# Rotary embedding in a hybrid decoder trunk: blocks of rows moved to other partitions by ScalarE copies instead of transfers

## The chip, the cores and the metric

The program runs on one core of a Trainium2 chip. The core has five engines, each with a queue of its own that is worked through in order: TensorE (PE in the profile: matmuls, and PEld for its weight loads), VectorE (DVE), ScalarE (ACT), GpSimd (POOL) and SyncE (SP). An engine's queue can hold instructions that issue a transfer (DMA); here SP issues the loads of weights and ACT issues the small transfers inside the on-chip memory. On-chip data lie in 128 partitions (rows). The metric is the device time of one execution in microseconds (us), as the median of several runs.

## The reference

The reference is two layers of a decoder trunk with three branches side by side, on 512 tokens of width 1024 in float32. Each layer norms its input, projects it, runs the three branches (a chunked state-space scan, a latent attention, a gated delta rule), merges them through gates and an output projection, and ends in a feed-forward block. The change touches the latent attention alone:

```
def apply_rope(t, cos, sin):
    t1, t2 = tf[..., :half], tf[..., half:]          # half = 32 of 64 rotary channels
    return concat([t1 * cos - t2 * sin, t2 * cos + t1 * sin])

q = (rmsnorm(cq) @ w_uq).reshape(B, S, 8, 128 + 64)  # 8 heads, 128 plain and 64 rotary channels
q_nope, q_pe = split(q);  q_pe = apply_rope(q_pe, cos, sin)
k_nope, v = split(rmsnorm(ckv) @ w_ukv);  k_pe = apply_rope(k_rope, cos, sin)   # one k_pe for all heads
sc = einsum(q_nope, k_nope) + einsum(q_pe, k_pe)     # scaled, causal, then softmax and the product with v
```

## The kernel before

**Layout.** The attention works on transposed tiles: channels on the 128 partitions, the 512 tokens along the row. Every matmul operand is kept as a high and a low part (`hi` rounded to the matmul's input type, `lo` the rest), and each product is three matmuls (lines 181 to 183). ACT makes `hi` with a cast (line 159 for weights, line 256 for values out of PSUM), DVE makes `lo` with a subtraction (lines 160 and 257).

**The stage.** In each of the two layers the attention begins after the projections of the compressed query and key/value (`latent`, whose casts are line 260 and whose scaling is line 495), and runs over four head pairs `hp` (lines 540 to 651). The 64 rotary channels of the two heads of a pair lie together in one tile of 128 partitions: head 0 in partitions 0 to 63, head 1 in 64 to 127. A pair goes through these steps:

- `dense_F(q_weights(), ...)`, line 558: queries of the pair in three PSUM banks, `pp` being the rotary one. ACT scales it into `qp` (line 575), and the plain ones into `qh` (line 568).
- `rope(qp)`, line 576, gives `qr`, the rotated query.
- `qd` (lines 578 to 580) is `qr` with its two halves of 64 partitions exchanged: two transfers.
- `qps[j]`, for each head j of the pair, holds the rounded query of this head in both halves of the partitions: its own half is cast from `qr` (line 584), the other half from `qd` (line 586). `qpl[j]` holds the low part in its own half (DVE, line 585) and zero in the other.
- Keys `kh`, `kl` and values `vh`, `vl` of the pair (lines 587 to 596): matmuls into PSUM, then casts on ACT (line 256) and subtractions on DVE (line 257), which set the PSUM banks free. There are four banks of the kind `acc`, shared with the next pair's queries and with the other stages.
- For each head, four score blocks of 128 tokens: three plain matmuls (lines 607 to 609), the rotary matmul of `qps[j]` with `kps` (line 610), that of `qpl[j]` with `kph` (line 611), and the mask (line 612). `kps` holds the high part of the rotated key in partitions 0 to 63 and its low part in 64 to 127, so line 610 computes two products at once; this is why the query has to lie in both halves. Then the maximum (line 616), the exponential (line 619), transposes (line 629), and the products with the values (lines 645 to 647) into `yt`, whose cast is `yh` (line 256).

**The key.** Before the pairs, the 64 rotary channels of the shared key `smT` are doubled into `kd` (lines 520 to 522, two transfers), rotated by `rope(kd)` (line 523), and split into `kph` and `kps` (lines 526 to 528).

**`rope`**, lines 509 to 518: `sw_` is the source with neighbouring blocks of 32 partitions exchanged, made by four transfers (line 513); then DVE computes `ta = src * cosT`, `sw_ = sw_ * sinT` and their sum (lines 515 to 517). It runs five times in a layer.

**Buffers.** `kd`, `sw_`, `ta` and `qd` are tiles of a pool `mix` of eight buffers, which the probabilities of the attention (lines 632 and 633) use too.

**Order.** The kernel's text gives no order between engines, and not the final order on an engine. A planner simulates the program with costs of its own and puts each instruction into its engine's queue when it takes it to be ready, the earlier one in the text first; blocks under `high_priority` count as earlier in the text than they stand. The waits between engines follow from the data. So the transfers of lines 513, 522 and 580 stand in ACT's queue between casts, where the planner put them, and an instruction of that queue that has to wait holds up what is behind it.

Of the kernel before, what the change touches and what calls it, by code (L numbers as in the profile page):

```python
# [10 lines left out]
F32 = mybir.dt.float32  # L11
# [9 lines left out]
P = 128  # L21
S = 512
# [37 lines left out]
def hybrid_kernel(ctx, tc, a, out, depth=2, taps=None):  # L60
    nc = tc.nc
    pe, act, dve, pool, sync = nc.tensor, nc.scalar, nc.vector, nc.gpsimd, nc.sync
    uid = itertools.count()

    def mk(pl, shape, dt, tag, bufs=None):
        return pl.tile(shape, dt, tag=tag, name=f"{tag}_{next(uid)}", bufs=bufs)
# [5 lines left out]
    def f32(ap):  # L72
        return ap.bitcast(F32)
# [12 lines left out]
    lp = ctx.enter_context(tc.tile_pool(name="lp", bufs=1))  # L86
# [76 lines left out]
    def weights(w2d, c0, n, K, hold=None):  # L163

        kt = min(1024 // n, K // P)
        step = 512 // n
        for k0 in range(0, K // P, kt):  # L170
            raw = mk(wp, [P, kt * n], F32, "wraw", 2)
            sync.dma_start(raw.rearrange("p (k n) -> p k n", n=n),
                           w2d[k0 * P : (k0 + kt) * P, c0 : c0 + n].rearrange("(k p) n -> p k n", p=P))
            for q in range(0, kt, step):
                hi, lo = split_half(raw[:, q * n : (q + step) * n], hold and hold[k0 + q])
                v = lambda x: x.rearrange("p (k n) -> p k n", n=n)
                yield k0 + q, v(hi), v(lo)
# [158 lines left out]
    for ly in range(depth):  # L336
# [32 lines left out]
        smT = mk(ml, [96, S], F32, "qp")  # L369
# [139 lines left out]
        def rope(src):  # L509

            sw_ = mk(lp, [P, S], F32, "mix", 8)
            for i in range(4):
                act.dma_start(sw_[32 * i : 32 * i + 32], src[32 * (i ^ 1) : 32 * (i ^ 1) + 32])
            ta = mk(lp, [P, S], F32, "mix", 8)
            dve.tensor_tensor(ta, src, cosT, ALU.mult)
            dve.tensor_tensor(sw_, sw_, sinT, ALU.mult)
            dve.tensor_tensor(ta, ta, sw_, ALU.add)
            return ta

        kd = mk(lp, [P, S], F32, "mix", 8)  # L520
        for i in range(2):
            act.dma_start(kd[64 * i : 64 * i + 64], smT[:64])
        kpe = rope(kd)
        kph = mk(ml, [P, S], F32R, "kph")
        kps = mk(ml, [P, S], F32R, "kps")
# [14 lines left out]
        for hp in range(4):  # L540
# [33 lines left out]
            qp = mk(ml, [P, S], F32, "qp")  # L574
            act.mul(qp, pp, scale)
            qr = rope(qp)

            qd = mk(lp, [P, S], F32, "mix", 8)
            for i in range(2):
                act.dma_start(qd[64 * i : 64 * i + 64], qr[64 * (1 - i) : 64 * (1 - i) + 64])  # L580
            qps = [mk(ml, [P, S], F32R, f"qps{j}") for j in range(2)]
            for j in range(2):
                half, other = (slice(64 * i, 64 * i + 64) for i in (j, 1 - j))
                act.copy(qps[j][half], qr[half])
                dve.tensor_tensor(qpl[j][half], qr[half], f32(qps[j][half]), ALU.subtract)
                act.copy(qps[j][other], qd[other])
            wkv = list(weights(a["mla_w_ukv"][ly], hp * 512, 512, 256))
            with tc.high_priority(30):
                ks = head_tiles(dense_F(wkv, [slice(0, P), slice(256, 256 + P)], 256, ckh, ckl), "k")
# [684 lines left out]
```

## Time and profile before

| | |
|---|---|
| median of 3 runs | 2353.61 us (2350.84 to 2354.39) |
| profiled execution | 2356.2 us |
| its span, from the first to the last instruction | 2354.4 us |
| mean granted TensorE clock | 0.998 of full speed |
| PE busy | 2309.5 us |
| DVE busy | 1608.8 us |
| ACT busy | 1154.9 us |
| attention of layer 0 and of layer 1, about | 60 to 205 us and 1222 to 1365 us of the span |

The profile shows one execution. An instruction is named by engine, line, operation and `out<-in` by tile names. A row of a timeline has its start and its duration in us, and in brackets how long the engine was idle before it and who released it. ACTq rows are instructions that ACT's sequencer handles itself, such as issuing a transfer. In the chain that ended last, each row is a start, a length and what the time was spent on. In a row for a line of the kernel, the three durations are the smallest, the median and the largest in ns. Matmuls are pipelined, so the busy time of PE says that it was not waiting, not that it ran at its peak.

### The profile page before, as it was taken

The page shows a single profiled execution, that of the slowest core. Times are in us where ns is not written, and L with a number is a line of the kernel's source. Part 1 is how long each engine was busy: PE and PEld are TensorE (multiplying, and loading weights), DVE is VectorE, ACT ScalarE, POOL GpSimd, SP SyncE. Part 2 cuts the span into 40 slices and gives each one's busy share as a digit, 9 for nine tenths or more (in the row PEclk, how much of TensorE's full clock was granted, in tenths as well). Part 3 has the DMA queues.
Part 4 walks back from the last instruction along what each step waited for, and adds up shares of the span by engine and source line. Part 5 has one row for each costly group of instructions (what it writes and reads, how often), then busy time and mean ns, then how long its engine had stood idle before and what let it go on. Part 6 is the DMA issues. An engine that isn't in the chain of part 4 may idle for free.

```text
span 2354.4 us, 32073 instructions
## 1 busy us (share of the span) xinstructions
PE 2309.5 (98%) x11972; PEld 1897.4 (81%) x11972; DVE 1608.8 (68%) x3184; ACT 1154.9 (49%) x2305; POOL 58.4 (2%) x76
## 2 busy tenths in 40 slices
PE   8999999999999999999999999999999999999998
PEld 7778788878887888888887787888888878888886
DVE  6776756775675458767757767667756645677668
ACT  6665434534453345544656553444435534455545
POOL 0000000000000000000000000000000000000000
PEclk9999999999999999999999999999999999999999
DMA  4222232252222443233132222323422224333231
GB/s 136 85 63 72 66 96 72 76 148 72 72 63 72 143 152 101 71 125 117 50 99 65 72 81 63 93 69 99 126 79 65 63 81 157 129 108 107 90 108 45
DMA packets 194172, 215.16 MB, mean 91 GB/s; under 512 B 32352, under 2 KB 153696, under 8 KB 194016
## 3 DMA queue, kind: packets, MB, share of 16 engines
q1 hardware_dynamic: 190496, 207.87, 29.0%
q10 hardware_dynamic: 3520, 5.25, 0.9%
q8 instruction: 94, 1.54, 0.3%
q14 instruction: 62, 0.51, 0.1%
HBM read 200.50 MB, written 7.34 MB: 88 GB/s over the span
## 4 chain that ended last, share of the span: by engine, by line
PE 90%; DVE 5%; DMA 2%; ACT 1%; issue 1%; POOL 1%; SPq 0%; DVEq 0%; POOLq 0%; ACTq 0%
PE acc L181 23%; PE acc L182 23%; PE acc L183 22%; PE sm L181 2%; PE sm L183 2%; PE sm L182 2%; PE sm L724 1%; DVE wlo L160 1%; PE sm L629 1%; PE yt L182 1%; PE yt L183 1%; PE yt L181 1%; PE sm L989 1%; DMA mix<-mix 1%; PE sm L461 1%
## 5 line engine op out<-in xcount | busy, mean ns | idle before, releaser
L160 DVE TENSOR_TENSOR wlo<-wraw,whi 128x512 fp32r<-128x512 f32 x552 | 378.3, 688 | 404.8 <-ACT whi L159 397.7
L159 ACT CAST whi<-wraw 128x512 fp32r<-128x512 f32 x552 | 342.0, 621 | 624.5 <-PE acc L182 406.6
L181 PE MATMUL acc<-xh,whi 128*128 128x512 f32 (+1 forms) x1184 | 462.1, 391 | 2.2 <-DVE vl L257 2.2
L183 PE MATMUL acc<-xh,wlo 128*128 128x512 f32 (+1 forms) x1184 | 459.3, 388 | 0.0
L182 PE MATMUL acc<-xl,whi 128*128 128x512 f32 (+1 forms) x1184 | 459.3, 388 | 0.0
L181 PEld LDWEIGHTS acc<-xh,whi 128*128 128x128 f32 x1184 | 222.8, 189 | 44.4 <-DVE vl L257 2.8
L182 PEld LDWEIGHTS acc<-xl,whi 128*128 128x128 f32 x1184 | 223.0, 188 | 42.6 <-issue 1.0
L183 PEld LDWEIGHTS acc<-xh,wlo 128*128 128x128 f32 x1184 | 222.9, 188 | 41.9 <-issue 0.5
L181 PE MATMUL acc<-yh,whi 128*128 128x512 f32 x384 | 153.1, 402 | 0.0
L182 PE MATMUL acc<-yl,whi 128*128 128x512 f32 x384 | 152.3, 397 | 0.0
L183 PE MATMUL acc<-yh,wlo 128*128 128x512 f32 x384 | 151.4, 394 | 0.0
L183 PE MATMUL acc<-whi,xl 128*128 128x512 f32 (+1 forms) x384 | 144.0, 375 | 0.0
L181 PE MATMUL acc<-whi,xh 128*128 128x512 f32 (+1 forms) x384 | 143.4, 375 | 0.0
L182 PE MATMUL acc<-wlo,xh 128*128 128x512 f32 (+1 forms) x384 | 143.2, 373 | 0.0
L665 DVE SCALAR_TENSOR_TENSOR cva<-acc,pc,cva 128x511 f32<-128x511 f32 (+2 forms) x168 | 120.1, 742 | 16.7 <-ACT cva L661 9.5
L159 ACT CAST whi<-wr 128x512 fp32r<-128x512 f32 x128 | 79.5, 621 | 68.2 <-PE acc L183 32.7
L182 PE MATMUL acc<-wlo,yh 128*128 128x512 f32 x256 | 99.7, 390 | 0.0
L181 PE MATMUL acc<-whi,yh 128*128 128x512 f32 x256 | 99.7, 389 | 0.0
L183 PE MATMUL acc<-whi,yl 128*128 128x512 f32 x256 | 99.7, 389 | 0.0
L160 DVE TENSOR_TENSOR wlo<-wr,whi 128x512 fp32r<-128x512 f32 x128 | 85.8, 685 | 12.5 <-ACT whi L159 11.7
L181 PEld LDWEIGHTS acc<-yh,whi 128*128 128x128 f32 x384 | 71.6, 188 | 16.9 <-ACT yh L260 2.2
L182 PEld LDWEIGHTS acc<-yl,whi 128*128 128x128 f32 x384 | 72.2, 188 | 16.0 <-issue 1.9
(381 smaller groups left out, 4601.3 us busy)
## 6 DMA issues: line engine op xcount, KB each, us to landing
wraw<-in_w_in_dram SPq DMA_DIRECT2D x148, 512.0 KB, 3.6
wraw<-in_w_up_dram SPq DMA_DIRECT2D x64, 512.0 KB, 3.6
wr<-in_w_down_dram SPq DMA_DIRECT2D x32, 1024.0 KB, 5.0
wraw<-in_w_mla_out_dram SPq DMA_DIRECT2D x16, 512.0 KB, 3.4
wraw<-in_w_ssd_out_dram SPq DMA_DIRECT2D x16, 512.0 KB, 3.4
wraw<-in_w_gdn_out_dram SPq DMA_DIRECT2D x16, 512.0 KB, 3.3
wraw<-in_w_out_dram SPq DMA_DIRECT2D x16, 512.0 KB, 3.6
wraw<-in_mla_w_uq_dram SPq DMA_DIRECT2D x16, 384.0 KB, 3.4
```

The lines of the kernel that those rows point to most:

```text
L159: act.copy(hi, raw)
L160: dve.tensor_tensor(lo, raw, f32(hi), ALU.subtract)
L181: pe.matmul(o, ah, bh, start=start, stop=False, skip_group_check=more)
L182: pe.matmul(o, ah, bl, start=False, stop=False, skip_group_check=more)
L183: pe.matmul(o, al, bh, start=False, stop=stop, skip_group_check=more)
L461: pe.matmul(ps, w, cum[1][:, t].rearrange("p i l -> p (i l)"), start=True, stop=True)
L629: pe.transpose(ps[:, n : n + P], pn[t][:, kb * P : (kb + 1) * P], ident)
L665: dve.scalar_tensor_tensor(acc[:, d:], ps[:, : S - d], taps_[3 - d], acc[:, d:], ALU.mult, ALU.add)
L724: pe.matmul(py[:, h * 64 : (h + 1) * 64], e2[h // 4][:, h % 4, :], xd[:, h * 64 : (h + 1) * 64], start=True, stop=True)
L989: pe.matmul(po[:, h * P : (h + 1) * P], pt_[:, h, :], vn[:, h * P : (h + 1) * P], start=True, stop=True)
```

## The change

The four transfers of the exchange in `rope`, and the two that double the key, become copies on ACT with the same source and destination. `qd` goes away with its two transfers; the other half of `qps[j]` is now cast straight from `qr`, from the half of the partitions in which the head lies to the other.

```diff
@@ rope(src)
             sw_ = mk(lp, [P, S], F32, "mix", 8)
             for i in range(4):
-                act.dma_start(sw_[32 * i : 32 * i + 32], src[32 * (i ^ 1) : 32 * (i ^ 1) + 32])
+                act.copy(sw_[32 * i : 32 * i + 32], src[32 * (i ^ 1) : 32 * (i ^ 1) + 32])
             ta = mk(lp, [P, S], F32, "mix", 8)
...
         kd = mk(lp, [P, S], F32, "mix", 8)
         for i in range(2):
-            act.dma_start(kd[64 * i : 64 * i + 64], smT[:64])
+            act.copy(kd[64 * i : 64 * i + 64], smT[:64])
         kpe = rope(kd)
...
             qr = rope(qp)
 
-            qd = mk(lp, [P, S], F32, "mix", 8)
-            for i in range(2):
-                act.dma_start(qd[64 * i : 64 * i + 64], qr[64 * (1 - i) : 64 * (1 - i) + 64])
             qps = [mk(ml, [P, S], F32R, f"qps{j}") for j in range(2)]
             for j in range(2):
                 half, other = (slice(64 * i, 64 * i + 64) for i in (j, 1 - j))
                 act.copy(qps[j][half], qr[half])
                 dve.tensor_tensor(qpl[j][half], qr[half], f32(qps[j][half]), ALU.subtract)
-                act.copy(qps[j][other], qd[other])
+                act.copy(qps[j][other], qr[half])
```

## The prediction

> **What bounds the kernel now.** I read the page first: the engines' busy time and the chain that ended last.
>
> ```profile
> span 2354.4 us, 32073 instructions
> PE 2309.5 (98%) x11972; PEld 1897.4 (81%) x11972; DVE 1608.8 (68%) x3184; ACT 1154.9 (49%) x2305; POOL 58.4 (2%) x76
> PE 90%; DVE 5%; DMA 2%; ACT 1%; issue 1%; POOL 1%; SPq 0%; DVEq 0%; POOLq 0%; ACTq 0%
> ```
>
> TensorE sets the time: 2354.4 - 2309.5 leaves 45 us in which it is idle. The change takes no matmul away, so all that it can win lies in those 45 us. Next I read the list of what PE waited for (total us, times, longest), then the five waits of its second line in PE's own timeline (start, duration; in brackets the idle time before and who ended it).
>
> ```profile
> PE sm L296 <- DVE xr L291: 9.0, 2, 8.7
> PE sm L610 <- ACT qps L586: 5.3, 5, 1.9
> PE acc L181 <- DVE vl L257: 3.6, 4, 1.1
> ...
> 115.69 0.38 PE L610 MATMUL sm<-kps,qps 128*128 128x256 f32 x1 [0.56 <-ACT qps L586]
> 146.72 0.39 PE L610 MATMUL sm<-kps,qps 128*128 128x256 f32 x1 [1.08 <-ACT qps L586]
> 1251.43 0.39 PE L610 MATMUL sm<-kps,qps 128*128 128x256 f32 x1 [1.13 <-ACT qps L586]
> 1282.63 0.39 PE L610 MATMUL sm<-kps,qps 128*128 128x256 f32 x1 [1.89 <-ACT qps L586]
> 1314.78 0.39 PE L610 MATMUL sm<-kps,qps 128*128 128x256 f32 x1 [0.62 <-ACT qps L586]
> ```
>
> The second-largest wait of the kernel is the one that the change touches: the rotary score matmul of a head pair waits for the copy that reads the doubled query. The five are 0.56 + 1.08 + 1.13 + 1.89 + 0.62 = 5.28 us. The chain, followed through these places, names what lay behind the copy.
>
> ```profile
> 110.73 4.28 DMA mix<-mix
> 140.10 5.21 DMA wraw<-in_w_in_dram
> 1246.18 4.56 DMA mix<-mix
> 1276.33 5.61 DMA mix<-mix
> 1308.61 4.75 DMA wraw<-in_w_in_dram
> ```
>
> Three times it is the doubling transfer itself, twice a load of weights. Why a load of weights: the last copy L586 then stands on ACT behind a weight cast L159 that waits for it. After the longest wait PE also ran at a lower clock; the table of windows (length, then PE's busy time and so on, the granted clock after POOL) shows it beside the same matmuls in layer 0.
>
> ```profile
> 1283.38:1287.13 3.75, 3.75 (x13) 2.50 (x12) 2.58 (x11) 1.60 (x6) 0.00 (x0) 0.54 0.00 0
> 116.63:118.78 2.15, 2.15 (x12) 1.50 (x12) 2.03 (x10) 1.60 (x6) 0.00 (x0) 1.00 0.00 0
> ```
>
> At 0.54 of full clock the stretch took 3.75 us, at 1.00 2.15 us: 1.60 us lost behind the 1.89 us idle, none behind the shorter ones. [...]
>
> **The change, part by part.** *Transfers removed:* per layer 2 (doubling the key) + 5 x 4 (swaps in the rotary helper) + 4 x 2 (doubled query) = 30, in two layers 60.
>
> ```profile
> q10 hardware_dynamic: 3520, 5.25, 0.9%
> L513 ACTq DMA_DIRECT2D mix<-qp x32: 514/552/613, 74.3 to 1335.3; - x32
> DMA to landing us min/median/max: 2.2/2.6/5.6
> 140.28 1.50 ACTq L580 DMA_DIRECT2D mix<-mix  x1
> ```
>
> These 60 are the whole queue q10 (5.25 MB). An issue holds ACT's sequencer for 552 ns (median); the landing row is that of the doubled query, median 2.6 us, worst 5.6 us, and the first of the two late weight loads (140.10 to 145.31) had one issued beside it at 140.28. *Copies added:* 22 per layer, 44 in all, of 32 or 64 partitions by 512.
>
> ```profile
> L447 ACT CAST cw<-wk x4: 615/616/617, 241.1 to 1410.1; 32x512 fp32r<-32x512 f32 x4
> L584 ACT CAST qps<-mix x16: 615/617/623, 82.1 to 1340.9; 64x512 fp32r<-64x512 f32 x16
> 112.23 0.62 ACT L159 CAST whi<-wraw 128x512 fp32r<-128x512 f32 x1 [1.42 <-PE acc L182]
> 112.75 1.26 ACT L584 CAST qps<-mix 64x512 fp32r<-64x512 f32 x2
> ```
>
> No row copies to other partitions than it reads. The nearest, at 32 and at 64 partitions, take 0.616 us, so 44 x 0.617 = 27 us more ACT work (1155 to 1182 us). Bounds for one: 0.52 us, the distance of the whole-tile cast at 112.23 to the next, and twice the row, 1.23; I take 0.63, since two copies of different halves took 1.26. [...] ACT is at 49%, so 27 us matter only where PE waits for what is queued behind a copy.
>
> *The copy L586 (same count, other source).* It now waits for DVE's sum L517 only, like L584 before it. Where the order stays as it is, the four copies run back to back.
>
> ```profile
> 1278.36 1.26 ACT L584 CAST qps<-mix 64x512 fp32r<-64x512 f32 x2
> 145.40 0.62 ACT L159 CAST whi<-wraw 128x512 fp32r<-128x512 f32 x1 [1.10 <-DMA wraw<-in_w_in_dram]
> ```
>
> From 1278.36 four at 0.63 end at 1280.9; PE came free at 1282.63 - 1.89 = 1280.74, so about 0.2 us of that wait stays, and likewise 112.75 + 2.52 = 115.27 against 115.13. At 1251.43 it goes wholly. In the two waits behind the weight cast (146.72, 1314.78) the planner had set the last copy behind it because of the transfer; with no transfer of 2.6 us behind the query I expect it ahead. Gain: 5.28 + 1.60 - 0.4 = 6.5 us. Late next is PE's wait for the value split `vl`.
>
> *The copies in the rotary helper.* They replace issues in the same in-order queue, so they stand before the same instructions, but hold the engine where an issue held the sequencer only. What is behind them on ACT and awaited by PE are the casts of keys (`kh`), values (`vh`) and head outputs (`yh`), which release PSUM banks.
>
> ```profile
> 70.90:80.60 9.70, 9.06 (x55) 7.92 (x55) 9.00 (x22) 7.48 (x23) 0.00 (x0) 1.00 0.33 106
> 66.92 0.69 ACT L260 ACTIVATE ckh<-sm,pc 128x512 fp32r<-128x512 f32 x1 [2.83 <-PE sm L500]
> 73.63 0.60 ACT L575 ACTIVATE qp<-acc 128x512 f32<-128x512 f32 x1
> 74.82 0.59 ACT L256 CAST kh<-acc 128x512 fp32r<-128x512 f32 x1 [0.59 <-PE acc L183]
> 76.74 0.27 ACT L256 CAST vh<-acc 128x128 fp32r<-128x128 f32 x1 [0.30 <-PE acc L183]
> 77.55 0.85 ACT L256 CAST vh<-acc 128x128 fp32r<-128x128 f32 x4 [0.54 <-PE acc L183]
> 79.03 0.47 PE L181 MATMUL acc<-cqh,whi 128*128 128x512 f32 x1 [0.64 <-DVE vl L257]
> 1243.48 0.47 PE L181 MATMUL acc<-cqh,whi 128*128 128x512 f32 x1 [0.78 <-DVE vl L257]
> 71.54 1.37 DVE L569 SCALAR_TENSOR_TENSOR ql<-acc,qh 128x512 fp32r<-128x512 f32 x2 [1.89 <-ACT qh L568]
> 72.83 0.68 DVE L516 TENSOR_TENSOR mix<-mix,sinT 128x512 f32<-128x512 f32 x1
> 105.91 0.59 ACT L256 CAST yh<-yt 128x512 fp32r<-128x512 f32 x1 [1.80 <-PE yt L647]
> 168.81 0.50 PE L181 MATMUL acc<-xh,whi 128*128 128x512 f32 x1 [1.08 <-DVE vl L257]
> ```
>
> First pair of a layer: four copies are 2.52 us, ACT's idle there 0.59 + 0.30 + 0.54 = 1.43, so `vh` could slip by up to 1.09 us. Against that, DVE is the fuller engine (9.00 of 9.70 us), and the key's swap arrives late in it: L516 at 72.83 and the sum after it, some 1.3 us, could run in the 1.89 us that DVE idles before 71.54, once the key's swap is six copies (3.8 us) instead of two rounds of transfers. I set this pair at nothing, with -1.4 us (0.64 + 0.78 won) and +2.2 us as ends. Cover gone, it costs the 2.2. The other three pairs: the issues stand in front of the `yh` cast of the pair before, in idle ACT time; three copies (1.9 us) fill it and the fourth can delay one cast by up to 0.62. I take a quarter of that, 0.15 x 6 = 0.9 us, ends 0 and 3.7. The key's six copies at the layer's start lie in idle ACT time such as the 2.83 us before 66.92: nothing taken; without that cover one delays a latent cast by 0.62 in each layer, 1.2 us.
>
> *Buffers:* `mix` tiles per pair fall from 11 to 10 over 8 buffers; nothing quoted here waits for one, so nothing; a late one would hold a copy just as it held the issue in its place.
>
> **Sum.** -6.5 + 0.9 = -5.6 us. The profiled execution took 2356.2 us (span 2354.4), 2.6 over the median 2353.61; 2350.6 by it, and on the median 2348.0.
>
> **The rivals.**
> *The order keeps the copies where they were* (the change does not do what it says): the two waits behind weight casts stay, 1.08 + 0.62. -5.6 + 1.7 = -3.9: 2349.7. For it: 145.40 stands on a load, not on the doubling. Against: that place in the queue came with the transfer.
> *The dip stays*, caused by something other than the idle gap: the 1.60 us are not won, -5.6 + 1.6 = -4.0: 2349.6. For it: four of the five waits, up to 1.13 us, have no dip in the rows seen. Against: it begins within 0.8 us of the end of the longest. [...]
> *A wait in place of the other:* each of six pairs delays a cast by one whole copy, and each layer's start too: 3.7 + 1.2 = 4.9, so -6.5 + 4.9 = -1.6: 2352.0. For it: PE already waits on `vl` four times. Against: ACT is idle about half the time.
> *Slower: the copies go ahead of the value casts.* At the first pair `vh` slips by 1.09 in both layers (2.2 us); at the other six the excess of four copies over the idle before `yh` is taken as 0.7, so 4.2. That is 6.4, and eats the gain; it turns the sign at 0.8 us per pair (6.5 / 8). PE's idle then is 0.64 + 1.09 = 1.73, 0.78 + 1.09 = 1.87 and 1.08 + 0.7 = 1.8 twice, near the 1.89 behind which a dip cost 1.60: four dips, 6.4. Result -6.5 + 6.4 + 6.4 = +6.3: 2359.9. For it: the in-order queue and the four `vl` waits. Against: DVE, not ACT, is the fuller engine there.
>
> **How the numbers follow.** What a measurement can tell from no change is about 0.2%, 4.7 us: below 2348.9 faster, above 2358.3 slower. Forecast 0.48 (of it 0.07 ends just above 2348.9), order kept 0.11, dip stays 0.06, new wait 0.10, slower 0.21 and 0.04 outside (an order reshuffled in later stages, 0.02 faster, 0.01 and 0.01). Faster 0.41 + 0.02 = 0.43, same 0.07 + 0.11 + 0.06 + 0.10 + 0.01 = 0.35, slower 0.22. The forecast's own range is 2345 to 2350 (ends of its terms: -1.4 at the first pairs, other pairs 0 or doubled). The range to state runs from 2343 (all of it, and the first pair's 1.4, with 2 us of spread in the median) to 2361 (the slower case with 1 us more).
>
> **What would show it.** Right: q10 gone; line 513 as a copy of some 0.62 us on ACT, its busy time near 1182; no wait of L610 on L586; clock 1.00 throughout the second attention stage; L516 earlier. Wrong: `vl` waits longer than 3.6 us in all, ACT casts with a copy as the instruction before, or copies slower than 0.63.

## The result, and the profile after

| | before | after |
|---|---|---|
| median of 5 runs | 2351.92 us (2350.84 to 2354.39) | 2366.33 us (2363.86 to 2367.94) |
| ratio | | 1.0056, 95% interval 1.0045 to 1.0067 |
| profiled execution | 2356.2 us | 2363.86 us |

The change makes the kernel slower by 0.56%, against a forecast of 2348.0 us and a range that ended at 2361. The profiled execution of after is the fastest of its five, and that of before is slower than the five runs of before. So the two profiles show 7.7 us of the 14 us between the medians. In the other runs of after the mean granted clock was 0.996 or 0.997 (0.998 in the profiled one); below it is shown what lowers it in the profiled one. Of the executions behind the later sections, one of late_double and two of before took 5239 to 8175 us each, and the medians and ratios leave these three out.

The page of after, with the busy times and the chain:

```profile
span 2362.1 us, 31972 instructions
PE 2312.3 (98%) x11972; PEld 1896.8 (80%) x11972; DVE 1606.9 (68%) x3184; ACT 1179.9 (50%) x2349; POOL 58.5 (2%) x76
PE 88%; DVE 5%; ACT 4%; POOL 1%; DMA 1%; issue 1%; SPq 0%; DVEq 0%; POOLq 0%; ACTq 0%
```

ACT's share of the chain went from 1% to 4%, that of DMA from 2% to 1%. The transfers became copies, and the copies are now part of what sets the end. The queue q10 is gone from the page. Line 513 (in after, lines from 578 on stand three lower than in before: the rotary score is L607, the `qps` casts are L581 and L583):

```profile
L513 ACT COPY mix<-qp x32: 615/618/621, 74.9 to 1338.2; 32x512 f32<-32x512 f32 x32
L513 ACT COPY mix<-mix x8: 615/617/622, 65.4 to 1235.6; 32x512 f32<-32x512 f32 x8
```

From the list of what PE waited for, the two rows that make up most of the attention's (total us, times, longest):

```profile
PE sm L607 <- ACT qps L583: 8.3, 7, 3.8
PE acc L181 <- DVE vl L257: 7.6, 6, 1.8
```

Before, the same rows were 5.3 us in 5 and 3.6 us in 4. The wait that the change was to remove has grown, and the one next to it has doubled. PE's timeline says where (start, duration, and in brackets the idle time before):

```profile
111.53 0.47 PE L181 MATMUL acc<-cqh,whi 128*128 128x512 f32 x1 [1.79 <-DVE vl L257]
112.86 0.39 PE L607 MATMUL sm<-kps,qps 128*128 128x256 f32 x1 [0.17 <-ACT qps L583]
142.13 0.47 PE L181 MATMUL acc<-cqh,whi 128*128 128x512 f32 x1 [1.79 <-DVE vl L257]
170.66 0.33 PE L606 MATMUL sm<-kh,ql 128*128 128x384 f32 x1
174.75 0.39 PE L607 MATMUL sm<-kps,qps 128*128 128x256 f32 x1 [3.76 <-ACT qps L583]
...
1279.87 0.47 PE L181 MATMUL acc<-cqh,whi 128*128 128x512 f32 x1 [1.80 <-DVE vl L257]
1310.55 0.47 PE L181 MATMUL acc<-cqh,whi 128*128 128x512 f32 x1 [1.79 <-DVE vl L257]
1343.17 0.39 PE L607 MATMUL sm<-kps,qps 128*128 128x256 f32 x1 [3.75 <-ACT qps L583]
```

Two places, each in both layers. In the second and third pair a query matmul of the next pair waits 1.8 us for a PSUM bank that the value split `vl` has to free. In the last pair the plain scores end (170.66) and the rotary score follows with nothing between: 3.76 us idle. ACT's timeline shows what both waited behind:

```profile
105.46 0.60 ACT L575 ACTIVATE qp<-acc 128x512 f32<-128x512 f32 x1
...
106.56 2.51 ACT L513 COPY mix<-qp 32x512 f32<-32x512 f32 x4
109.09 0.77 ACT L256 CAST vh<-acc 128x128 fp32r<-128x128 f32 x4
...
166.73 0.61 ACT L575 ACTIVATE qp<-acc 128x512 f32<-128x512 f32 x1
...
167.84 2.51 ACT L513 COPY mix<-qp 32x512 f32<-32x512 f32 x4
...
171.42 0.76 ACT L256 CAST vh<-acc 128x128 fp32r<-128x128 f32 x4
172.96 0.62 ACT L581 CAST qps<-mix 64x512 fp32r<-64x512 f32 x1 [0.78 <-DVE mix L517]
174.09 0.62 ACT L583 CAST qps<-mix 64x512 fp32r<-64x512 f32 x1
```

The four copies stand as a block of 2.51 us in front of the value casts `vh`, and in the last pair they are part of an 8.02 us path from `qp` (166.73) to the rotary score (174.75).

The table of windows over the two attention stages (between the same marks in both kernels: to the first cast of L447, in layer 1 from the last transpose of L500, in layer 0 from 9.4 us ahead of it), and over the matmuls behind the two long waits (length, PE busy and so on; the clock is the number after POOL):

```profile
174.80:179.80 5.00, 5.00 (x19) 3.97 (x20) 3.66 (x13) 2.80 (x9) 0.00 (x0) 0.66 0.13 46
1343.20:1347.50 4.30, 4.30 (x16) 3.40 (x17) 3.61 (x13) 2.81 (x9) 0.00 (x0) 0.60 0.15 54
58.30:248.40 190.10, 179.52 (x960) 145.13 (x959) 133.81 (x312) 121.10 (x286) 1.54 (x2) 0.99 0.21 60
1236.00:1417.80 181.80, 173.66 (x926) 140.76 (x925) 127.17 (x292) 113.81 (x270) 0.53 (x1) 0.99 0.21 60
```

```profile
57.30:241.10 183.80, 177.49 (x961) 145.29 (x960) 134.60 (x312) 108.76 (x265) 1.54 (x2) 1.00 0.26 76
1230.80:1410.10 179.30, 173.31 (x926) 141.81 (x925) 127.97 (x291) 104.48 (x251) 0.52 (x1) 0.99 0.26 74
```

The first fence is after, the second before. The attention takes 190.1 + 181.8 = 371.9 us after and 183.8 + 179.3 = 363.1 us before: 8.8 us more. The waits for `qps` grew by 3.0 us and those for `vl` by 4.0. The slow matmuls behind the two long waits cost 5.00 x 0.34 + 4.30 x 0.40 = 3.4 us, where before lost 1.6 in such a place: 1.8 more. That is 8.8 us in all: the profiled loss lies in the attention and nearly all of it in these three things (the rest of the span is 1.1 us shorter than before). That the sum is met to the digit is partly chance: by the windows PE is idle 6.4 us longer, 18.7 against 12.3, where the two rows give 7.0, and busy 2.4 us longer for the same matmuls, where the slow stretches give 1.8.

What changed in the order is how many matmuls the planner puts between a pair's plain scores and its first rotary score; they are called its cover below. In the order of TensorE's instructions these are, for the four pairs of a layer:

```
before   29  30  35  33
after     5   4   4   0
```

In the first three pairs they are query matmuls of the next pair, in before with one to three key matmuls among them; in the last they are matmuls of the next stage. (The expectations below give for before and its like the unbroken run of query matmuls alone, 27, 27, 28 and 33; the numbers that they give for before_vals and late_vals differ from the table below by up to 7. The table counts every matmul in between, from the traces.)

### The profile page after: what moved, and what is told of

Same layout as the page of the kernel before. It is cut to its first block, busy times and chain, and to the rows that moved or that the text cites. A ratio compares the mean times of both kernels' runs of the same rounds, so it can differ in the third digit from the quotient of the medians.

```text
span 2362.1 us, 31972 instructions
## 1 busy us (share of the span) xinstructions
PE 2312.3 (98%) x11972; PEld 1896.8 (80%) x11972; DVE 1606.9 (68%) x3184; ACT 1179.9 (50%) x2349; POOL 58.5 (2%) x76
## 4 chain that ended last, share of the span: by engine, by line
PE 88%; DVE 5%; ACT 4%; POOL 1%; DMA 1%; issue 1%; SPq 0%; DVEq 0%; POOLq 0%; ACTq 0%
PE acc L181 22%; PE acc L182 22%; PE acc L183 22%; PE sm L182 2%; PE sm L181 2%; PE sm L183 2%; PE sm L721 1%; DVE wlo L160 1%; ACT mix L513 1%; PE sm L626 1%; PE yt L182 1%; PE yt L183 1%; PE yt L181 1%; PE sm L986 1%; PE yt L642 1%
```

## The experiments

Theory 1: the order changed. Where transfers had to be covered, the planner had put a query projection between plain and rotary scores; without them it takes `qps` to be ready early, moves the rotary score up, and the copies stand uncovered. Theory 2: the copies' own time on ScalarE, in front of what TensorE waits for, wherever they stand. Theory 3 was formed after the first eight runs: a copy costs what it is exposed for, and the two kinds of place seen above make up the whole loss.

| run | matmuls of cover, four pairs | median us | ratio to before, 95% interval |
|---|---|---|---|
| key_only | 25 29 35 33 | 2356.17 | 1.0012 (1.0003 to 1.0022) |
| swap_only | 17 15 17 6 | 2360.59 | 1.0030 (1.0018 to 1.0042) |
| qd_only | 15 15 15 0 | 2364.07 | 1.0047 (1.0034 to 1.0061) |
| early_q | 0 36 36 13 | 2368.96 | 1.0070 (1.0056 to 1.0084) |
| extra_late | 27 31 34 33 | 2358.25 | 1.0021 (1.0011 to 1.0031) |
| early_q_late_rope | 36 36 36 12 | 2356.73 | 1.0018 (1.0009 to 1.0027) |
| before_early | 36 36 36 33 | 2355.71 | 1.0012 (1.0004 to 1.0021) |
| late_rope | 12 16 4 20 | 2348.36 | 0.9983 (0.9974 to 0.9991) |
| late_last | 5 4 4 14 | 2359.77 | 1.0033 (1.0021 to 1.0045) |
| late_rest | 12 16 4 0 | 2360.30 | 1.0031 (1.0019 to 1.0043) |
| before_late | 42 40 39 35 | 2368.04 | 1.0069 (1.0057 to 1.0080) |
| vals_first30 | 11 16 16 18 | 2349.70 | 0.9988 (0.9979 to 0.9996) |
| late_double | 18 17 16 29 | 2356.45 | 1.0016 (1.0007 to 1.0025) |
| no_swap | 1 1 1 0 | 2351.14 | 0.9991 (0.9982 to 1.0000) |
| before_vals | 45 40 39 35 | 2369.32 | 1.0072 (1.0060 to 1.0084) |
| late_vals | 16 24 19 29 | 2351.33 | 0.9989 (0.9980 to 0.9998) |

The ratios go with the runs of before that were made beside each; their medians were 2352.62 to 2353.16 us.

### One part of the change alone

key_only: only the key's 12 copies.

```diff
-        def rope(src):
+        def rope(src, move):
-                act.dma_start(sw_[32 * i : 32 * i + 32], src[32 * (i ^ 1) : 32 * (i ^ 1) + 32])
+                move(sw_[32 * i : 32 * i + 32], src[32 * (i ^ 1) : 32 * (i ^ 1) + 32])
-            act.dma_start(kd[64 * i : 64 * i + 64], smT[:64])
+            act.copy(kd[64 * i : 64 * i + 64], smT[:64])
-        kpe = rope(kd)
+        kpe = rope(kd, act.copy)
-            qr = rope(qp)
+            qr = rope(qp, act.dma_start)
```

> Copies on ACT only for the key (its doubling and its swap, 12 of the 44 copies); the query's swap and doubling stay transfers. The order on PE is nearly that of before: 25, 27 and 28 query matmuls of the next pair, and 33 of the next stage, between a pair's plain scores and its rotary ones (before 27, 27, 28 and 33; after 5, 4, 4 and 0). Theory 1 (the loss comes from the changed order on PE): within 2 us of before. Theory 2 (the loss comes from the copies' time on ACT in front of what PE waits for): 12 of 44 copies, so 12/44 of 14 us, +4 us.

Measured: 0.12% slower, 3 us, with a cover close to before's. It lies between what the two theories gave and separates neither.

swap_only: only the change of line 513, so 40 copies; both doublings stay transfers.

```diff
-                act.dma_start(sw_[32 * i : 32 * i + 32], src[32 * (i ^ 1) : 32 * (i ^ 1) + 32])
+                act.copy(sw_[32 * i : 32 * i + 32], src[32 * (i ^ 1) : 32 * (i ^ 1) + 32])
```

> Copies on ACT for the swap alone (40 of the 44), doubling of key and query stay transfers. Order on PE: 17, 15, 17 and 6 matmuls of cover. Theory 1: half the cover is gone and the last pair has little, while the doubling transfer is still behind the swap: slower by 5 to 15 us, most of it as waits of the last pair's rotary scores. Theory 2: 40 of 44 copies, +13 us, as waits for the value casts in every pair.

qd_only: only the doubled query without `qd`. No copy is added anywhere.

```diff
-            qd = mk(lp, [P, S], F32, "mix", 8)
-            for i in range(2):
-                act.dma_start(qd[64 * i : 64 * i + 64], qr[64 * (1 - i) : 64 * (1 - i) + 64])
-                act.copy(qps[j][other], qd[other])
+                act.copy(qps[j][other], qr[half])
```

> No copy added at all: the swap and the key stay transfers, only the doubled query is cast straight from the rotated one. Order on PE: 15, 15, 15 and 0 matmuls of cover. Theory 1: the last pair of each layer has no cover and waits for swap transfers and sum, 3 to 6 us each, the waits for the doubling transfer go: slower by 0 to 8 us. Theory 2: no copies, so faster by up to 5 us.

Measured: swap_only +0.30%, qd_only +0.47%. The waits of swap_only, then those of qd_only:

```profile
PE acc L181 <- DVE vl L257: 9.6, 6, 3.1
PE sm L610 <- ACT qps L586: 2.2, 2, 1.3
```


```profile
PE sm L607 <- ACT qps L583: 8.6, 4, 4.5
PE acc L181 <- DVE vl L257: 3.5, 7, 0.8
```

For swap_only 7 us came: theory 1's range (5 to 15) holds and theory 2's 13 does not. But the waits are of theory 2's kind, for `vl` and hardly for `qps`; the two longest, 3.12 and 3.13 us, are those of a matmul of the next stage in the last pair.

Removing 16 transfers and adding nothing loses at least as much as the 40 copies (the two intervals overlap). In qd_only it is the same 8-odd us for `qps` as in after, with the largest (4.55 and 3.72 us) again in the last pair, where the cover is 0. No copy is there to blame, so theory 2 falls as the whole cause; that the order changes for the worse when only latency is taken out is shown. Theory 1 had 0 to 8 us for it and 11 came. Part of the excess is the clock: at each of the two long waits it stood at half for 6.83 us, which is 6.8 us lost in all where before lost 1.7.

```profile
170.66:177.49 6.83, 5.04 (x17) 3.74 (x18) 5.52 (x19) 4.61 (x13) 0.00 (x0) 0.50 0.13 44
1341.43:1348.26 6.83, 5.62 (x19) 4.23 (x20) 5.50 (x16) 4.04 (x14) 0.00 (x0) 0.50 0.17 59
```

### The query matmuls earlier

early_q: after, with the cover put back by priority.

```diff
-            *pq, pp = dense_F(q_weights(), tiles(384), 512, cqh, cql)
+            with tc.high_priority(300 if hp else 0):
+                *pq, pp = dense_F(q_weights(), tiles(384), 512, cqh, cql)
```

> The changed kernel with all 44 copies, and the next pair's query projection put ahead of the attention of the pair before in the planner's eyes (priority 300 instructions earlier). Order on PE: 36, 36, 36 and 13 matmuls of cover. Theory 1: the waits of the first three pairs go, the last pair has 13 matmuls (3 us) of cover: 10 to 20 us faster than the changed kernel, 0 to 8 us faster than the kernel before. Theory 2: as slow as the changed kernel, +14 us.

```profile
PE acc L181 <- DVE vl L257: 8.2, 6, 1.9
PE sm L608 <- ACT qps L584: 7.7, 2, 3.9
```

Theory 1's number failed: 2369 us, 16 above before, is nearer to theory 2's 14. The two long waits went to the first pair (3.87 us at 83.02, 3.84 at 1253.30), where the planner now set one rotary score ahead of the query matmuls, and those for `vl` stayed. In the first pair the 36 matmuls are no cover, since they stand behind that score, and in the others cover does nothing for the casts behind the copies.

The same edit on the kernel before, where the transfers stay:

> Before, with only the higher priority of the query matmuls: transfers kept, 36, 36, 36 and 33 matmuls in front of the rotary score (before: 27, 27, 28, 33). If the rest of the waits for qps in before is cover that is too short by a few matmuls (each 0.23 us, so 8 more are 1.8 us, and the waits are 1.8 us and less), it is 2345 to 2350 us; if the query matmuls then wait for value splits instead, it is 2352 to 2362 us.

Measured +0.12%, as the second expectation had it: the waits for `qps` are gone from the list and those for `vl` went from 3.6 us in 4 to 7.1 us in 8. One wait was turned into the other.

### The copies' own time, and the block's place

extra_late: before, with four copies per pair that nobody reads, in an order of TensorE that stays nearly as it was (27 31 34 33 matmuls of cover for 29 30 35 33).

```diff
             dense_T(wkv, 256, 256, ckh, ckl, ev, lambda w: w.rearrange("p (h n) -> p h n", h=2)[:, :, P:])
+            jk_ = mk(ml, [P, S], F32, "jk_")
+            for i in range(4):
+                act.copy(jk_[32 * i : 32 * i + 32], qp[32 * (i ^ 1) : 32 * (i ^ 1) + 32])
```

> Before, with four copies of 32 rows per pair added on ScalarE, written behind the value matmuls, into a tile that nobody reads (32 copies, 0.62 us each, 20 us of ScalarE); every transfer stays, and so does the order of the matmuls (27, 27, 28 and 33 matmuls between a pair's plain scores and its first rotary score, as before). Theory 1 (what costs is the changed order on TensorE): 2351 to 2356 us, waits as before. Theory 2 (what costs is the copies' own time on ScalarE, in front of what TensorE waits for): 2357 to 2362 us.

Measured +0.21%, 5 us: theory 2's number. So 32 copies cost about 0.15 us each with the order nearly kept, and theory 1 falls as the whole cause too. Where these 5 us lie is not shown: in the two profiled executions the attention is only 1.6 us longer (364.7 against 363.1), and 1.9 us of the other 2.4 are TensorE's wait at the very start (L296, 10.9 against 9.0), which no copy touches.

late_rope: after, with the text from `qr = rope(qp)` to the last copy of `qps` moved behind the value matmuls, so that the value casts count as earlier than the copies.

```diff
-            qr = rope(qp)
...
-                act.copy(qps[j][other], qr[half])
             wkv = list(weights(a["mla_w_ukv"][ly], hp * 512, 512, 256))
...
             dense_T(wkv, 256, 256, ckh, ckl, ev, lambda w: w.rearrange("p (h n) -> p h n", h=2)[:, :, P:])
 
+            qr = rope(qp)
...
+                act.copy(qps[j][other], qr[half])
```

> After, with only the rotary block written behind the value matmuls: every copy stays; 12, 16, 4 and 20 matmuls in front of the rotary score (after: 5, 4, 4, 0), and the value casts ahead of the copies. Theory 1: between after and before, 2353 to 2361 us, with the waits for vl gone and those for qps left where 4 matmuls stand. Theory 2: 2360 to 2367 us.

Measured 2348.36 us, ratio 0.9983 (0.9974 to 0.9991): faster than both kernels, with every copy in place, and better than either theory said. Its waits for the two rows, then ACT's and PE's timelines of the last pair:

```profile
PE acc L181 <- DVE vl L257: 3.0, 4, 0.9
PE sm L607 <- ACT qps L594: 0.5, 2, 0.3
```

```profile
163.29 0.63 ACT L575 ACTIVATE qp<-acc 128x512 f32<-128x512 f32 x1
163.86 0.27 ACT L256 CAST vh<-acc 128x128 fp32r<-128x128 f32 x1
164.15 1.25 ACT L513 COPY mix<-qp 32x512 f32<-32x512 f32 x2
165.43 0.43 ACT L256 CAST vh<-acc 128x128 fp32r<-128x128 f32 x2
...
167.43 1.25 ACT L513 COPY mix<-qp 32x512 f32<-32x512 f32 x2
```

```profile
166.58 0.34 PE L606 MATMUL sm<-kh,ql 128*128 128x384 f32 x1
166.75 0.39 PE L181 MATMUL acc<-xh,whi 128*128 128x512 f32 x1
...
171.74 0.38 PE L607 MATMUL sm<-kps,qps 128*128 128x256 f32 x1 [0.26 <-ACT qps L594]
```

The copies stand between value casts instead of ahead of them. The path from `qp` to the rotary score is no shorter than in after (171.74 - 163.29 = 8.45 us against 8.02), nor does `qp` come earlier before the last plain scores (3.3 us against 3.9). The difference is that 20 matmuls of the next stage fill the 5 us behind them, and 0.26 us is left of 3.76. What counts here is not the path but what stands beside it. The number of matmuls alone does not give the wait either: the third pair has 4 of them, as in after, and no wait over 0.3 us for `qps`.

early_q_late_rope puts both edits together:

> After, with the query matmuls of pairs 1 to 3 of a layer at a higher priority and the rotary block written behind the value matmuls: every copy stays on ScalarE, but 36, 36, 36 and 12 matmuls stand between plain scores and rotary score, in the first pair too, and the value casts are issued ahead of the copies. Theory 1: 2347 to 2355 us, the 3.8 us waits for qps and the 1.8 us waits for vl both under 1 us. Theory 2 (the copies' time as such): stays at 2360 to 2367 us, as the copies are all there.

Measured +0.18%, 2356.73 us, between the two ranges. The waits for `qps` are gone, as theory 1 said; those for `vl`, which it had under 1 us, are 10.1 us in 8, the longest 1.8. So the place of the block recovers most, and forcing the query matmuls early on top gives 8 us of it away.

### The two places apart

late_last moves the block behind the value matmuls for `hp == 3` alone; TensorE's order in the other three pairs stays that of after. late_rest does it for `hp < 3`.

```diff
+            def rotate():
+                qr = rope(qp)
...
+                return qps
+
+            if hp < 3:
+                qps = rotate()
             wkv = list(weights(a["mla_w_ukv"][ly], hp * 512, 512, 256))
...
+            if hp == 3:
+                qps = rotate()
```

> After, with the rotary block written behind the value matmuls in the last pair of a layer alone; the order of the matmuls in the other three pairs stays as in after, and in the last pair 14 matmuls of the next stage stand between plain scores and rotary score where after has none. Theory 3 (a place costs what its copies are exposed for, and two kinds of place make up the whole loss): the two waits of 3.76 and 3.75 us for qps go, and the slow matmuls behind them, about 1 us each; the four waits of 1.8 us for vl stay: 2355 to 2360 us. Theory 2 (the copies' time as such): 2363 to 2368 us.

> The mirror of the last: the rotary block behind the value matmuls in the first three pairs, and ahead of the key matmuls, as in after, in the last pair (12, 16, 4 and 0 matmuls of cover). Theory 3: the four waits of 1.8 us for vl go or fall under 1 us, the two of 3.8 us for qps stay: 2355 to 2360 us, and its gain and that of the last pair alone add up to the 18 us of the block moved in all four. Theory 2: 2363 to 2368 us.

Measured 2359.77 and 2360.30 us: the first within theory 3's range, the second 0.3 us beyond it. That the two gains add up failed: in the medians they are 6.6 and 6.0 us, 12.6 of the 18.0 that all four pairs give. The windows of the attention stages, late_last, late_rest and late_rope in this order:

```profile
58.10:244.20 186.10, 178.20 (x960) 144.00 (x960) 133.66 (x312) 121.00 (x286) 1.54 (x2) 1.00 0.21 61
1232.70:1413.00 180.30, 175.04 (x926) 141.89 (x925) 127.27 (x292) 113.91 (x270) 0.52 (x1) 0.98 0.21 61
```

```profile
56.80:243.60 186.80, 178.99 (x961) 145.51 (x960) 134.99 (x312) 121.97 (x287) 1.54 (x2) 0.99 0.21 61
1231.60:1411.00 179.40, 174.05 (x926) 141.85 (x925) 128.25 (x292) 114.51 (x269) 0.52 (x1) 0.98 0.21 61
```

```profile
57.50:239.60 182.10, 177.68 (x961) 143.98 (x960) 134.61 (x312) 121.70 (x287) 1.54 (x2) 1.00 0.22 62
1227.90:1401.50 173.60, 171.69 (x926) 139.48 (x925) 127.82 (x292) 114.37 (x270) 0.53 (x1) 1.00 0.22 63
```

PE's idle time (length less busy) is 18.7 us in after, 13.2 in late_last, 13.2 in late_rest and 6.3 in late_rope: gains of 5.6 and 5.6, of 12.4, so the waits nearly add up. What does not is PE's busy time for the same matmuls: 353.2, 353.2 and 353.0 us, and 349.4 only where both waits are gone. That is the clock, which late_last and late_rest still lose, most of it in layer 1 (0.98).

### Whose place it is

vals_first30 leaves the text of after and gives the value matmuls and their casts the priority of the keys. late_vals does both moves.

```diff
-            dense_T(wkv, 256, 256, ckh, ckl, ev, lambda w: w.rearrange("p (h n) -> p h n", h=2)[:, :, P:])
+            with tc.high_priority(30):
+                dense_T(wkv, 256, 256, ckh, ckl, ev, lambda w: w.rearrange("p (h n) -> p h n", h=2)[:, :, P:])
```

> After, with the value matmuls and their casts at a higher priority (30, as the keys have), the text of the rotary block unmoved: 11, 16, 16 and 18 matmuls of cover in front of the rotary score (after: 5, 4, 4, 0). Theory 3: 2347 to 2355 us, no wait for qps over 1 us, those for vl under 1 us. Theory 2: 2360 to 2367 us.

> After with both moves, the rotary block behind the value matmuls and the values at priority 30: 10, 24, 19 and 29 matmuls of cover. If both moves take away the same exposed copies: 2346 to 2350 us, as each alone. If they add up: 2340 to 2346 us.

Measured 0.9988 and 0.9989: each move recovers the loss by itself, and the two do not add. Two details were missed: vals_first30 keeps two waits for `vl` of 1.5 us where theory 3 had under 1, and late_vals, at 2351.33 us, is 1.3 us above the range for either expectation. The same two edits on the kernel before:

> Before, with the rotary block and its transfers written behind the value matmuls. If the place of the block is what gains, whoever moves the rows: 2344 to 2350 us, with the 5.3 us of waits for qps gone. If the later place helps only where ScalarE does the copying, since there it takes the copies from in front of the value casts: 2351 to 2357 us.

> Before, with the value matmuls at priority 30: transfers kept, and 46, 47, 46 and 33 query and key matmuls of cover. If cover is what counts, whoever moves the rows: 2344 to 2350 us. If more cover than the transfers need only pushes work behind the softmax, as with the rotary block and its transfers moved (there 8.3 us of the transposes' waits came): 2353 to 2366 us.

Measured 1.0069 and 1.0072: 2368.04 us, 11 above both expectations for before_late, and 2369.32 us, 3 above the second for before_vals. The moves that gain 16 to 17 us with the copies lose 16 to 17 us with the transfers. In before_late the cover is some 40 matmuls and the waits went on:

```profile
PE sm L629 <- DVE pn L621: 8.3, 12, 1.0
PE sm L610 <- ACT qps L596: 2.4, 2, 1.3
```

The transposes L629 wait for the softmax. The reading is that so much stands ahead of the late rotary score that nothing is left to cover the softmax behind it; no run tests that by itself. Theory 3 had not said this. It means that copies against transfers is no question with one answer: at the text's first place the transfers are better by 0.56%, at the later place the copies by 0.9% (1.0069 / 0.9983).

### What a copy costs where it has cover

late_double adds four unread copies per pair to late_rope, just ahead of the rotary block; no_swap is after without the swap copies.

```diff
+            jk_ = mk(ml, [P, S], F32, "jk_")
+            for i in range(4):
+                act.copy(jk_[32 * i : 32 * i + 32], qp[32 * (i ^ 1) : 32 * (i ^ 1) + 32])
             qr = rope(qp)
```

> After with the rotary block behind the value matmuls, and four more copies of 32 rows per pair in front of it, into a tile that nobody reads: 32 more copies, 20 us more of ScalarE, and 18, 17, 16 and 29 matmuls of cover (without them 12, 16, 4 and 20). Theory 3 (a copy costs what it is exposed for): 2347 to 2351 us, no wait for qps over 1 us. Theory 2 (a copy costs its time on ScalarE, wherever it stands): 2354 to 2362 us.

```diff
-            for i in range(4):
-                act.copy(sw_[32 * i : 32 * i + 32], src[32 * (i ^ 1) : 32 * (i ^ 1) + 32])
-            dve.tensor_tensor(sw_, sw_, sinT, ALU.mult)
+            dve.tensor_tensor(sw_, src, sinT, ALU.mult)
```

> After without its 32 query swap copies and 8 key swap copies: the sine term is taken from the rows as they are, so the rotary embedding is wrong. 1, 1, 1 and 0 matmuls of cover. Theory 3: what a pair has to wait for is shorter by four copies, 2.5 us, so the 3.75 us waits fall to about 1.3 us and the vl waits of 1.8 us to under 1 us: 2347 to 2355 us. If the order alone costs, without anything long behind it: 2360 to 2368 us.

late_double came out at 1.0016, 0.33% or 8 us above late_rope, with the waits for `qps` at 2.7 us in 6: theory 3's number failed and theory 2's held. How much of the 8 us the copies cost is open, since not all of it lies where they stand: in the profiled executions the attention is 4.5 us longer (360.2 against 355.7), and the mean granted clock is 0.997 against 0.999 of late_rope; where it was lost is not shown.

no_swap came out at 0.9991, 0.65% or 15 us below after, with the long waits at 1.25 us as theory 3 had it: 40 copies at after's places cost 15 of their 25 us. The other expectation, that the order alone costs, failed (2351 us, not 2360 to 2368): with 0 or 1 matmuls of cover the kernel is as fast as before, as its path to the rotary score is shorter by the four copies. So neither the lost cover nor the copies make the loss alone; it is what stands on that path with nothing beside it, transfers in qd_only and copies in after. What one copy costs depends on its place, and the place is the planner's.

## Why the prediction was wrong

*Transfers removed, copies added: right.* q10 is gone, 40 of the 44 copies are the rows of line 513 at 0.615 to 0.622 us, four of them in 2.51 us (0.63 each, no overlap), and ACT went from 1154.9 to 1179.9 us (said: 1182).

*The copy L586, gain 6.5 us: half right.* In the first three pairs of both layers the waits for `qps` are 0.15 to 0.17 us or none, as computed (0.2), where before had 0.56 to 1.89. But the step took it that nothing else moves. In the last pair, which had no wait at all before, 3.76 and 3.75 us came.

*"They replace issues in the same in-order queue, so they stand before the same instructions": this is the step that failed.* The queue's order is not kept; the planner makes it anew from what it takes to be ready. In before the query's rotary half `qp` was evicted at 99.58 us, 6.3 us before the `yh` cast at 105.91, and its rotary score ran at 115.69, 16.1 us later. In after `qp` comes at 105.46, behind `yh` (102.87), and its rotary score 7.40 us later. The latency that was taken out had cost 5.3 us of waits and the 1.6 us dip, since 29 to 35 matmuls stood beside the rest; with the latency the planner dropped the cover too, and 0 to 5 matmuls are left. The prediction gave a reshuffled order 0.04, and in later stages, not here. qd_only shows the step alone: the doubling transfers go, no copy comes, the cover falls to 15, 15, 15 and 0, and 11 us are lost.

*First pair at nothing, ends -1.4 and +2.2: right.* The waits there fell from 0.64 and 0.78 to 0.23 and 0.22 us, a gain of 1.0. As said, the key's sum moved ahead into DVE's idle time: L517 at 70.80, where before even L516 stood at 72.83.

*Other pairs 0.9 us, ends 0 and 3.7: wrong in mechanism.* It weighed the copies against the idle time before `yh`. They stand behind `yh` now and ahead of `vh`: four waits of 1.79 or 1.80 us, 7.2 us in all. Two of the signs of being wrong that the prediction had named came: the `vl` waits are 7.6 us, above 3.6, and the `vh` cast at 109.09 stands right behind a copy.

*The slower rival (2359.9) had the mechanism, copies ahead of the value casts, and the size of one wait (1.73 to 1.87)*, but had it at the first pair and at the end of the layer, not in the second and third pair; it counted dips behind these waits, where the profiled run shows none; and it knew nothing of the last pair. Its price per dip, 1.6 us, was met by the two that came (1.7 each).

*The clock.* The prediction counted the dip of before as coming from the idle gap; a rival had another cause for it. In after a dip stands behind each of the gaps of 3.76 and 3.75 us (0.66 and 0.60), and none behind the four of 1.8 us (1.00). That 1.89 us in before had one behind it, while 1.94 and 2.00 us in key_only had none (last section), leaves the cause open. The prediction read the dip of before as beginning within 0.8 us of the gap's end; the trace's clock falls at 1283.64, 1.0 us behind it.

*The size.* In the terms of the sum, by the two profiles: the 6.5 us to be won at the copy L586 became 4.8 lost (the waits for `qps` 3.0, the clock 1.8), and the 0.9 us to be lost to `vl` became 4.0. The two profiles give 7.7 us; the ratio says 13. The rest is not in a trace. The granted clock of the runs of before was 0.9989 in the mean, where each run lists it; that of after 0.997. 0.002 of 2310 us of matmuls is 4.6 us, which would be most of it, but that is argued from means.

What stays open is why the planner covers as it does (in late_rope 16 matmuls in one pair and 4 in the next), and with it why the two remedies do not add up. No run changed the planner's costs.

## What to carry to other kernels

Before removing a latency, look at what stands beside it: as far as it is covered, its removal gains nothing, and a planner that no longer needs the cover may move the consumer up to where the new, shorter path is bare. After such a change compare the order of the bounding engine's instructions, not only busy times, and count what stands in front of each consumer. When work goes from a queue to an engine, put it in the text behind what releases the bounding engine's buffers; here that one move was worth 17 to 18 us and turned a loss of 0.56% into a gain of 0.17%. It goes with the copies: with the transfers the same move lost 16 us.

## What the runs showed of the hardware

The granted clock behind an idle gap of TensorE in the attention, from windows of 1.5 us over the 6 us behind each gap: behind 21 gaps of 1.08 to 1.61 us (four each in before and key_only, three in early_q_late_rope, two each in before_vals, before_late, vals_first30, late_double and no_swap) it was 1.00 in every window. Of ten gaps of 1.79 to 2.06 us, seven had 1.00 as well: the four of after, those of 1.94 and 2.00 us in key_only (at 86.67 and 1251.32) and one of 1.79 us in early_q_late_rope. Behind the other three it fell to 0.50: 1.89 us in before (1282.63), 2.06 us in before_vals (1260.34) and 1.79 us in early_q_late_rope. It fell to 0.50 behind the 3.76 and 3.75 us of after too, and at the two long waits of qd_only it stood at 0.50 for 6.83 us. The length of the gap alone does not tell the cases apart, as the two of 1.79 us in early_q_late_rope show (171.52 and 1337.47; length, busy times, clock after POOL):

```profile
171.52:173.02 1.50, 1.50 (x6) 1.28 (x7) 1.05 (x4) 0.42 (x1) 0.00 (x0) 0.91 0.00 0
173.02:174.52 1.50, 1.50 (x5) 1.13 (x5) 0.68 (x1) 1.43 (x3) 0.00 (x0) 0.50 0.00 0
174.52:176.02 1.50, 1.50 (x6) 1.22 (x4) 0.69 (x1) 0.48 (x1) 0.00 (x0) 0.50 0.00 0
176.02:177.52 1.50, 1.50 (x11) 1.16 (x11) 1.33 (x4) 1.16 (x5) 0.00 (x0) 0.95 0.00 0
1337.47:1338.97 1.50, 1.50 (x7) 1.25 (x8) 1.05 (x4) 0.42 (x1) 0.00 (x0) 1.00 0.00 0
1338.97:1340.47 1.50, 1.50 (x9) 1.27 (x7) 0.68 (x1) 1.44 (x3) 0.00 (x0) 1.00 0.00 0
```

Nor do shorter waits always go without: in before_late, behind waits of 1.00, 0.24 and 0.23 us close together (matmuls at 139.25, 140.25 and 140.98), the score matmuls of 128x256 start 0.21 or 0.22 us apart from 142.32 on and 0.12 or 0.13 us apart from 144.74 on. In late_last, whose order in the first three pairs is that of after, the clock was 1.00 over the attention of layer 0, and in layer 1 it was lower in the stretches of two of after's four waits of 1.8 us (length, busy times, clock after POOL):

```profile
1276.50:1282.50 6.00, 5.80 (x21) 4.34 (x22) 4.43 (x15) 4.10 (x13) 0.00 (x0) 0.72 0.00 0
1308.70:1313.20 4.50, 4.49 (x17) 3.49 (x18) 3.24 (x8) 3.51 (x11) 0.00 (x0) 0.62 0.02 4
```

What decides it was not shown; no run was made for it. In these ten cases a wait of about 2 us cost its length and, in three of them, 1.7 us on top (the windows' lengths times what their clock lacks of 1.00).

A copy on ACT from one block of partitions to another took the same time as the nearest rows without a move: 0.618 us for 32 partitions (L513, against 0.616 of L447), and 0.618 us for 64 (the casts L583, which read the other half, against 0.617 of L581, which do not).
